# A hybrid decoder trunk: attention two heads at a time between late projections, and the recurrent chain ahead of them

## The chip, the cores and the metric

The kernel runs on one core of a Trainium2 chip. The metric is device time in microseconds for one execution, the median of several runs. The profile is of one further execution. Its engines are TensorE (PE in the rows, PEld its weight loads), VectorE (DVE), ScalarE (ACT), GpSimd (POOL) and SyncE (SP), which here only issues DMAs.

## The reference, cut to what matters

Two layers on a residual stream x of 512 positions by 1024 channels, all in fp32:

```python
for l in range(2):
    x = x + 0.5 * swiglu_ffn(x, ...)            # 1024 -> 2816 -> 1024
    p = rms_norm(x, mix_norm[l]) @ w_in[l]      # split in four groups of heads
    y_a = pool_mixer(p_a, ...)                  # causal means over 2, 4, 8, 16 positions
    y_b = rwkv7_mixer(p_b, ...)                 # recurrence over the 512 positions, 4 heads of 64
    y_c = nsa_mixer(p_c, ...)                   # compressed, selected and windowed attention, 4 heads
    y_d = short_conv_mixer(p_d, ...)            # gated convolution of width 3
    x = x + concat[y_a, y_b, y_c, y_d] @ w_out[l]
    x = x + 0.5 * swiglu_ffn(x, ...)
```

With 512 positions all eight blocks of 64 are selected, so the selected and the windowed attention are both plain causal attention, with keys of their own.

## The kernel before

Activations lie with channels on the 128 partitions and positions along the free dimension. Every large matrix product takes fp32 operands as a high and a low part: `split` loads a weight tile of 128x1024, ScalarE casts it to the high part (L203), VectorE subtracts for the low part (L204), and `mm3` (L206) issues three matmuls of 128x128 by 512 columns for each of the eight chunks of 128 channels (L209 to L211). A weight load (L193) brings two such tiles into one of two buffers.

The feed-forward halves (`ffn`) are dense in such matmuls. The mixers stand between them. `tilep(i)` computes one of 21 projections of 128 output channels, 24 matmuls, into a PSUM bank, mostly one of the two "d" banks. The order of NAMES is: eight for the recurrence (0 to 7), five for attention (8 to 12), two for the pool (13, 14), six for the convolution (15 to 20).

The order of the instructions is made by a planner before the run: it simulates the engines and at each step issues, of the instructions that are ready in its simulation, the one with the lowest priority number. Numbers grow in the order of the program; `at(off, ...)` sets another start for what it calls. Each engine then works strictly in the planned order. The parts and where they stand in it:

- `Rwkv.prep` (L755), once for each half of the heads, prepares the recurrence, in program order.
- `solve` (L924) builds per chunk of 64 positions the triangular matrices M (L936, L938), sends them through DRAM (L944, L946), substitutes on VectorE (L953 to L958), sends the result back (L963, L968) and merges blocks with small matmuls (L983 to L1014), 32x32 and 64x64. Offset 0 from p0, which is the start of the mixers plus 600.
- `chain` (L813) goes through eight chunks one after another: matmuls L824 and L827, a copy on ScalarE (L830), L836, copies on ScalarE and VectorE (L837, L838), L846, and the new state on VectorE (L857). `out` (L861) normalizes four chunks and puts the result into the split output yh, yl (`put`, L452). Offsets 300 and 500.
- `nsa` (L508) prepares the attention, `compress` (L612) with its matmuls L623 among it. Then 32 units, (block of 128 queries, pair of heads j, head in the pair hp, branch br), go through `scores` (L540: matmul L545, minimum on VectorE L548, exponential on ScalarE L551, scaling on ScalarE L555) and, one unit later, `values` (L558: transposes L562, copy L564, matmuls L574). The last unit of a pair of heads puts its output (L577). Offset 2000.
- `filler` holds the pool and convolution projections (13 to 20) with their work and the splits of chunks 0, 1, 6 and 7. Offset 3000.

At the end the output projection (`mix`, L353 to L363) takes the eight chunks of yh, yl in order, while x is reloaded by DMAs on POOL's queue (L354).

Of the kernel before, what the change touches and what calls it, by code (L numbers as in the profile page):

```python
# [98 lines left out]
class Net:  # L99
    PRI = (0, 0, 300, 2000, 3000)  # L100
# [105 lines left out]
    def mm3(self, ps, wh, wl, xh, xl, n, first=True, last=True):  # L206
        for k in range(n):
            sl = slice(k * P, (k + 1) * P)
            self.nc.tensor.matmul(ps, wh[:, sl], xh[:, k], start=(first and k == 0), stop=False)  # L209
            self.nc.tensor.matmul(ps, wh[:, sl], xl[:, k], start=False, stop=False)  # L210
            self.nc.tensor.matmul(ps, wl[:, sl], xh[:, k], start=False, stop=(last and k == n - 1))  # L211
# [108 lines left out]
    def mix(self, h, win, wout, cmpk, cmpv, g):  # L320
# [61 lines left out]
    def mixers(self, tilep, cmpk, cmpv):  # L382
# [4 lines left out]
        p0 = base + 600  # L387
        PR = self.PRI
# [3 lines left out]
        def at(off, fn, *a):  # L392
            save = self.tc.cur_priority
            self.tc.cur_priority = p0 + off
# [4 lines left out]
        def take(i, ps):  # L399
# [7 lines left out]
            if "L0" in sh and "L1" in sh and "rw" not in st:  # L407
                st["rw"] = Rwkv(self, sh)
            for j in range(2):
                if all(n in sh for n in ("L0", "L1", f"k{j}", f"r{j}", f"v{j}")) and j not in st:  # L410
                    st[j] = 1
                    st["rw"].prep(j)
            if all(n in raw for n in ("KV", "q0", "q1", "KS", "VS")) and "L1" in sh and "u" not in st:
                st["u"] = at(PR[1], self.nsa, raw, sh["L1"], cmpk, cmpv) if PR[1] else self.nsa(raw, sh["L1"], cmpk, cmpv)
# [20 lines left out]
        at(PR[4], filler)  # L435

# [13 lines left out]
        self.tc.cur_priority = p0 + 10000  # L450

# [56 lines left out]
    def nsa(self, raw, L1, cmpk, cmpv):  # L508
# [31 lines left out]
        def scores(i, j, hp, br):  # L540
            w, h = P * (i + 1), 2 * j + hp
            hs = slice(64 * hp, 64 * hp + 64)
            kt = KS if br == hp else KW
            pq = self.pd()
            nc.tensor.matmul(pq[:, :w], Q[j][hs, i * P:(i + 1) * P], kt[hs, :w], start=True, stop=True)  # L545
            sc = self.ring()
            mx = self.small(1, "mx", bufs=4)
            nc.vector.tensor_tensor_reduce(sc[:, :w], pq[:, :w], c["bias"][:, S - w:S],  # L548
                                           -(2.0 ** (-2 * (h + 1))), 3.0e38, ALU.add, ALU.min, mx)
            sm = self.small(1, "sum", bufs=4)  # L550
            nc.scalar.activation(sc[:, :w], sc[:, :w], AF.Exp, bias=mx, scale=-1.0, accum_out=sm)  # L551
            cf = self.small(1, "cf", bufs=4)
            nc.vector.reciprocal(cf, sm)
            nc.vector.tensor_mul(cf, cf, gh[:, i, h, 1 + br:2 + br])
            nc.scalar.activation(sc[:, :w], sc[:, :w], AF.Copy, scale=cf)  # L555
            return sc

        def values(sc, i, j, hp, br):  # L558
            w = P * (i + 1)
            ptr = self.pn()  # L560
            for b in range(i + 1):
                nc.tensor.transpose(ptr[:, b * P:(b + 1) * P], sc[:, b * P:(b + 1) * P], self.ident)  # L562
            pT = self.ring()
            nc.scalar.copy(pT[:, :w], ptr[:, :w])  # L564
            if hp == 0 and br == 0:
# [13 lines left out]
        def run():  # L579
            prev = None  # L580
# [10 lines left out]
    def cmp_blocks(self, KV):  # L591
# [3 lines left out]
        for which in range(2):  # L595
# [9 lines left out]
            blk = self.mt(f"cblk{which}", [P, 16, 31])  # L605
# [6 lines left out]
    def compress(self, Q, cmpk, cmpv, gh):  # L612
        nc = self.nc
        v, c = self.v, self.c
        hid = []
        for which, src in ((0, cmpk), (1, cmpv)):
            blk = self.blocks[which]
            ph = self.pn()
            for l4 in range(4):
                w1 = self.ring()  # L620
                nc.sync.dma_start(w1, src[:, 4 * l4:4 * l4 + 4].rearrange("p a b -> p (a b)"))
                for l in range(4 * l4, 4 * l4 + 4):
                    nc.tensor.matmul(ph[0:31, 0:P], blk[:, l], w1[:, (l % 4) * P:(l % 4 + 1) * P],  # L623
                                     start=(l == 0), stop=(l == 15))
            x = self.mt("gx", [32, P])
            u = self.mt("gu", [32, P])
            nc.gpsimd.memset(x, 0.0)
            nc.scalar.copy(x[0:31], ph[0:31, 0:P])
            nc.vector.tensor_mul(u, x, x)
            nc.vector.tensor_scalar(u, u, GELU_A, 1.0, ALU.mult, ALU.add)  # L630
            nc.vector.tensor_mul(u, u, x)
            nc.scalar.activation(u, u, AF.Tanh, scale=GELU_B)
            nc.vector.tensor_scalar(u, u, 0.5, 0.5, ALU.mult, ALU.add)
            nc.vector.tensor_mul(u, u, x)
            pt = self.pn()
            nc.tensor.transpose(pt[:, 0:32], u, self.ident[0:32, 0:32])
            hT = self.mt(f"hT{which}", [P, 4, 32])
            for r in range(1 if which == 0 else 4):
                nc.scalar.copy(hT[:, r], pt[:, 0:32])
            hid.append(hT)  # L640
# [52 lines left out]
    def conv(self, j, tilep, i):  # L693
        nc = self.nc
        cw = self.v["conv"]
        pc = tilep(i)
        ct = self.uring()[:, :S]
        nc.vector.tensor_mul(ct, pc, self.rs)
        nc.gpsimd.tensor_mul(ct, ct, self.rs)
        pu = tilep(i + 1)  # L700
        z = self.uring()[:, :S + 2]
        nc.gpsimd.memset(z[:, 0:2], 0.0)
        nc.vector.tensor_mul(z[:, 2:], ct, pu)
        t = self.yt(6 + j)
        nc.scalar.activation(t, z[:, 0:S], AF.Copy, scale=cw[:, j:j + 1])
# [445 lines left out]
```

## Time and profile before

| | us |
|---|---|
| median of 3 runs | 2085.72 |
| lowest, highest | 2083.14, 2086.73 |
| the profiled execution | 2084.97 |
| its span, first to last instruction | 2083.2 |
| TensorE busy | 2057.5 (99%) |
| VectorE busy | 998.2 (48%) |
| ScalarE busy | 683.3 (33%) |
| GpSimd busy | 258.7 (12%) |

Matmuls are pipelined and their ends are modelled, so a row's duration is longer than the time to the next row's start; prices of matmuls are read here from start to start. A plain fp32 matmul shows two records, one of the split products shows one, a transpose one. The granted clock is a share of the full 2.4 GHz.

### The profile page before, as it was taken

How to read it: one execution, taken by the hardware profiler on the slowest of the kernel's cores; microseconds unless marked ns; L12 is line 12 of the kernel's file. 1: busy time of each engine (PE TensorE's matmuls, PEld its weight loads, DVE VectorE, ACT ScalarE, POOL GpSimd, SP SyncE). 2: the span in 40 equal slices, each digit the busy share in tenths (PEclk: the TensorE clock that was granted, in tenths of full speed). 3: DMA queues.
4: the chain of work that ended last, by engine and by line, in shares of the span. 5: the costliest groups of instructions: out<-in, count | busy, mean ns of one | idle time of the engine just before them, and what ended most of it. 6: DMA issues, size and time to landing. Idle time of an engine off the chain costs nothing.

```text
span 2083.2 us, 25358 instructions
## 1 busy us (share of the span) xinstructions
PE 2057.5 (99%) x10262; PEld 1660.9 (80%) x10262; DVE 998.2 (48%) x1792; ACT 683.3 (33%) x1101; POOL 258.7 (12%) x249
## 2 busy tenths in 40 slices
PE   8999999999999999999999999999999999999999
PEld 6888888778667888888888888887786688888887
DVE  5434445567555443443544344356674544344433
ACT  4322223331464322232333223233324643222221
POOL 1110111113001110011011001110130011100110
PEclk9999999999799999999999999999996999999999
DMA  5223223324103222322322232242250032223223
GB/s 197 94 90 104 100 89 129 117 68 111 63 1 102 90 101 84 109 101 82 110 95 88 87 108 98 84 144 86 92 129 22 1 101 101 94 84 114 86 91 98
DMA packets 60438, 195.20 MB, mean 94 GB/s; under 512 B 29344, under 2 KB 29472, under 8 KB 45600
## 3 DMA queue, kind: packets, MB, share of 16 engines
q1 hardware_dynamic: 57760, 185.18, 27.4%
q0 software_dynamic: 2560, 8.39, 1.1%
q8 instruction: 80, 1.31, 0.3%
q14 instruction: 38, 0.31, 0.0%
HBM read 183.58 MB, written 8.93 MB: 92 GB/s over the span
## 4 chain that ended last, share of the span: by engine, by line
PE 97%; DVE 2%; ACT 0%; issue 0%; DMA 0%; SPq 0%; DVEq 0%
PE d L209 15%; PE d L211 15%; PE d L210 15%; PE r L211 8%; PE r L209 8%; PE r L210 8%; PE n L211 5%; PE n L209 5%; PE n L210 5%; PE o L574 2%; PE d L545 2%; PE n L562 1%; PE r L936 1%; PE n L623 1%; PE c L827 1%; PE c L824 0%
## 5 line engine op out<-in xcount | busy, mean ns | idle before, releaser
L203 ACT CAST wh<-w 128x1024 fp32r<-128x1024 f32 (+2 forms) x360 | 344.3, 956 | 1086.4 <-issue 327.2
L204 DVE TENSOR_TENSOR wl<-w,wh 128x1024 fp32r<-128x1024 f32 (+2 forms) x360 | 400.7, 1113 | 218.5 <-ACT wh L203 211.5
L209 PE MATMUL d<-hh,wh 128*128 128x512 f32 x1008 | 396.9, 394 | 6.9 <-ACT hh L216 6.9
L210 PE MATMUL d<-hl,wh 128*128 128x512 f32 x1008 | 395.7, 393 | 2.7 <-DVE hl L217 2.7
L211 PE MATMUL d<-hh,wl 128*128 128x512 f32 x1008 | 394.9, 392 | 0.0
L210 PE MATMUL r<-hl,wh 128*128 128x512 f32 x736 | 287.0, 390 | 0.0
L211 PE MATMUL r<-hh,wl 128*128 128x512 f32 x736 | 286.8, 390 | 0.0
L209 PE MATMUL r<-hh,wh 128*128 128x512 f32 x736 | 286.8, 390 | 0.0
L270 POOL TENSOR_TENSOR al<-t,ah 128x512 fp32r<-128x512 f32 x88 | 152.6, 1734 | 1062.6 <-ACT ah L269 1062.6
L209 PEld LDWEIGHTS d<-hh,wh 128*128 128x128 f32 x1008 | 189.7, 188 | 49.9 <-ACT hh L216 6.9
L210 PEld LDWEIGHTS d<-hl,wh 128*128 128x128 f32 x1008 | 189.8, 188 | 44.2 <-DVE hl L217 5.3
L211 PEld LDWEIGHTS d<-hh,wl 128*128 128x128 f32 x1008 | 189.8, 188 | 41.3 <-issue 2.3
L264 DVE TENSOR_TENSOR t<-d,rs 128x512 f32<-128x512 f32 x88 | 60.5, 691 | 267.3 <-PE d L211 261.6
L268 DVE TENSOR_TENSOR t<-t,r 128x512 f32<-128x512 f32 x88 | 60.6, 688 | 220.9 <-PE r L211 220.7
L211 PEld LDWEIGHTS r<-hh,wl 128*128 128x128 f32 x736 | 138.2, 188 | 28.6
L209 PEld LDWEIGHTS r<-hh,wh 128*128 128x128 f32 x736 | 138.2, 188 | 28.6
L210 PEld LDWEIGHTS r<-hl,wh 128*128 128x128 f32 x736 | 138.2, 188 | 28.5
L211 PE MATMUL n<-ah,wl 128*128 128x512 f32 x352 | 137.1, 389 | 0.0
L209 PE MATMUL d<-ah,wh 128*128 128x512 f32 x352 | 137.1, 389 | 0.0
L209 PE MATMUL n<-ah,wh 128*128 128x512 f32 x352 | 137.0, 389 | 0.0
L210 PE MATMUL d<-al,wh 128*128 128x512 f32 x352 | 137.0, 389 | 0.0
L211 PE MATMUL d<-ah,wl 128*128 128x512 f32 x352 | 137.0, 389 | 0.0
(297 smaller groups left out, 2343.9 us busy)
## 6 DMA issues: line engine op xcount, KB each, us to landing
w<-in_g SPq DMA_DIRECT2D x87, 1024.0 KB, 4.8
w<-in_d SPq DMA_DIRECT2D x64, 704.0 KB, 4.0
w<-in_win SPq DMA_DIRECT2D x20, 1024.0 KB, 4.9
w<-in_wout SPq DMA_DIRECT2D x8, 1024.0 KB, 5.8
xd<-x POOLq DMA_DIRECT2D x16, 256.0 KB, 4.2
x<-xd POOLq DMA_DIRECT2D x16, 256.0 KB, 5.8
x<-in_x SPq DMA_DIRECT2D x8, 256.0 KB, 5.1
s<-in_cmpk SPq DMA_DIRECT2D x8, 256.0 KB, 3.4
```

The costliest lines, as they stand in the source:

```text
L203: self.nc.scalar.copy(hi, w)
L204: self.nc.vector.tensor_sub(lo, w, hi.bitcast(F32))
L209: self.nc.tensor.matmul(ps, wh[:, sl], xh[:, k], start=(first and k == 0), stop=False)
L210: self.nc.tensor.matmul(ps, wh[:, sl], xl[:, k], start=False, stop=False)
L211: self.nc.tensor.matmul(ps, wl[:, sl], xh[:, k], start=False, stop=(last and k == n - 1))
L264: nc.vector.tensor_mul(t, pg, self.rs)
L268: nc.vector.tensor_mul(th, th, pu)
L270: nc.gpsimd.tensor_sub(al, th, ah.bitcast(F32))
L545: nc.tensor.matmul(pq[:, :w], Q[j][hs, i * P:(i + 1) * P], kt[hs, :w], start=True, stop=True)
L562: nc.tensor.transpose(ptr[:, b * P:(b + 1) * P], sc[:, b * P:(b + 1) * P], self.ident)
L574: nc.tensor.matmul(po["o"][64 * hp:64 * hp + 64], VT[:, b, br * 64:br * 64 + 64], pT[:, b * P:(b + 1) * P], start=False, stop=(br == 1 and ...
L623: nc.tensor.matmul(ph[0:31, 0:P], blk[:, l], w1[:, (l % 4) * P:(l % 4 + 1) * P], start=(l == 0), stop=(l == 15))
```

## The change

It rearranges the mixers. The priorities: the recurrence's parts get offsets from -6000 to -3000 from the start of the mixers, so that they go ahead of all else that is ready; attention and the late projections get one common offset, 2600. The late projections are cut in eight pieces (two of the pool, three for each half of the convolution), and one piece stands behind every second unit of attention. A unit of attention is now two heads: 16 units, each with two score matmuls side by side (partitions 0 to 63 and 64 to 127, a "d" bank each) and values alternating between the two heads' output partitions. The scaling of the scores moves from ScalarE to VectorE. In `compress` the key and the value matmuls alternate, and their activation is computed once for both; in `solve` the two heads of a pair alternate. The outputs of attention and of the recurrence go to tiles of their own, in buffers used before for other things, and all are split at the end in the order 0, 1, 6, 7, 4, 5, 2, 3, in which the output projection takes them. The scratch rings "s" (4) and "u" (4) become one of 8.

```diff
-    def mm3(self, ps, wh, wl, xh, xl, n, first=True, last=True):
-        for k in range(n):
+    def mm3(self, ps, wh, wl, xh, xl, n, first=True, last=True, order=None):
+        for i, k in enumerate(order or range(n)):
...
-            self.mm3(ps, *w2, self.yh, self.yl, NCH)
+            self.mm3(ps, *w2, self.yh, self.yl, NCH, order=(0, 1, 6, 7, 4, 5, 2, 3))
...
-    PRI = (0, 0, 300, 2000, 3000)
+    EARLY, LATE = -6000, 2600
...
             if "L0" in sh and "L1" in sh and "rw" not in st:
-                st["rw"] = Rwkv(self, sh)
+                st["rw"] = at(self.EARLY, Rwkv, self, sh)
...
-                    st["rw"].prep(j)
+                    at(self.EARLY + 500 * (j + 1), st["rw"].prep, j)
...
-        at(PR[0], rw.solve)
-
-        def filler():
-            for j in range(2):
-                self.pool(j, tilep(13 + j))
-            for j in range(2):
-                self.conv(j, tilep, 15 + 3 * j)
-            self.yh = self.hp.tile([P, NCH, S], F32R, tag="hh", name=self.nm("yh"))
-            self.yl = self.hp.tile([P, NCH, S], F32R, tag="hl", name=self.nm("yl"))
-            for c in (0, 1, 6, 7):
-                self.put(c, slice(0, S), self.y[c])
-
-        at(PR[4], filler)
+        at(self.EARLY + 1500, rw.solve)
...
-        at(PR[2], chain, 0)
-        at(PR[2] + 200, chain, 1)
+        at(self.EARLY + 2500, chain, 0)
+        at(self.EARLY + 3000, chain, 1)

         def rest():
-            for _ in units:
-                pass
-
-        at(PR[3], rest)
+            pieces = [lambda: self.pool(0, tilep(13)), lambda: self.pool(1, tilep(14))]
+            for j in range(2):
+                pieces += self.conv(j, tilep, 15 + 3 * j)
+            for k, _ in enumerate(units):
+                if k % 2 == 0:
+                    pieces[k // 2]()
+            self.yh = self.hp.tile([P, NCH, S], F32R, tag="hh", name=self.nm("yh"))
+            self.yl = self.hp.tile([P, NCH, S], F32R, tag="hl", name=self.nm("yl"))
+            for c in (0, 1, 6, 7, 4, 5):
+                self.put(c, slice(0, S), self.y[c])
+            for g in range(2):
+                for c in (2, 3):
+                    self.put(c, slice(256 * g, 256 * g + 256), self.y[c][:, 256 * g:256 * g + 256])
+
+        at(self.LATE, rest)
...
+    def uring(self):
+        return self.mt("s", [P, 16 + S], bufs=8)
+
     def ring(self):
-        return self.mt("s", [P, S], bufs=4)
-
-    def uring(self):
-        return self.mt("u", [P, 16 + S], bufs=4)
+        return self.uring()[:, :S]
...
-        units = [(i, j, hp, br) for i in range(4) for j in range(2) for hp in range(2) for br in range(2)]
+        units = [(i, j, br) for i in range(4) for j in range(2) for br in range(2)]
...
+            pq = [self.pd(), self.pd()]
+            for hp in range(2):
+                hs = slice(64 * hp, 64 * hp + 64)
+                kt = KS if br == hp else KW
+                nc.tensor.matmul(pq[hp][:, :w], Q[j][hs, i * P:(i + 1) * P], kt[hs, :w], start=True, stop=True)
...
-            nc.scalar.activation(sc[:, :w], sc[:, :w], AF.Copy, scale=cf)
+                nc.vector.tensor_scalar(sc[:, :w], sc[:, :w], cf, None, ALU.mult)
...
             for b in range(i + 1):
-                nc.tensor.matmul(po["o"][64 * hp:64 * hp + 64], VT[:, b, br * 64:br * 64 + 64],
-                                 pT[:, b * P:(b + 1) * P], start=False, stop=(br == 1 and b == i))
-            if hp == 1 and br == 1:
-                self.put(4 + j, slice(i * P, (i + 1) * P), po["o"])
+                for hp in range(2):
+                    nc.tensor.matmul(po["o"][64 * hp:64 * hp + 64], VT[:, b, br * 64:br * 64 + 64],
+                                     pTs[hp][:, b * P:(b + 1) * P], start=False, stop=(br == 1 and b == i))
+            if br == 1:
+                nc.scalar.copy(self.y[4 + j][:, i * P:(i + 1) * P], po["o"])
...
+        ph = self.pn()
+        for l4 in range(4):
...
+            for l in range(4 * l4, 4 * l4 + 4):
+                for k in range(2):
+                    nc.tensor.matmul(ph[32 * k:32 * k + 31, 0:P], self.blocks[k][:, l],
+                                     w1[k][:, (l % 4) * P:(l % 4 + 1) * P], start=(l == 0), stop=(l == 15))
...
-        for j in range(2):
-            net.put(2 + j, ts_, t[:, 256 * j:256 * j + 256])
+        if g == 0:
+            self.y = net.mt("T16", [P, 2, S])
+            net.y[2], net.y[3] = self.y[:, 0], self.y[:, 1]
+        nc.vector.tensor_mul(self.y[:, :, ts_], t.rearrange("p (j s) -> p j s", j=2),
+                             pg.rearrange("p (j s) -> p j s", j=2))
...
-            for hp in range(2):
-                hs = slice(64 * hp, 64 * hp + 64)
-                for g in range(2):
-                    pm = net.pr()
-                    for i in range(4):
-                        ch = 4 * g + i
-                        nc.tensor.matmul(pm[:, i * P:(i + 1) * P], AK[j][hs, ch].rearrange("p a b -> p (a b)"),
+            for g in range(2):
+                pm = [net.pr(), net.pr()]
+                for i in range(4):
+                    ch = 4 * g + i
+                    for hp in range(2):
+                        hs = slice(64 * hp, 64 * hp + 64)
+                        nc.tensor.matmul(pm[hp][:, i * P:(i + 1) * P], AK[j][hs, ch].rearrange("p a b -> p (a b)"),
```

## Rows read from the trace of the kernel before

**Rows 1.** The page: busy times, granted clock by slice, the last chain.

```profile
PE 2057.5 (99%) x10262; PEld 1660.9 (80%) x10262; DVE 998.2 (48%) x1792; ACT 683.3 (33%) x1101; POOL 258.7 (12%) x249
PEclk9999999999799999999999999999996999999999
PE 97%; DVE 2%; ACT 0%; issue 0%; DMA 0%; SPq 0%; DVEq 0%
```

**Rows 2.** Busy time by stretch: us, engine busy (records), clock, DMA share, GB/s.

```profile
100.00:150.00 50.00, 50.00 (x222) 41.45 (x221) 18.98 (x24) 13.89 (x18) 6.75 (x4) 1.00 0.24 79
378.00:541.00 163.00, 158.88 (x956) 126.45 (x954) 109.88 (x232) 52.74 (x87) 30.06 (x52) 1.00 0.33 96
541.00:571.00 30.00, 29.00 (x252) 20.23 (x252) 12.52 (x55) 12.86 (x43) 0.00 (x0) 0.55 0.10 36
571.00:640.00 69.00, 68.31 (x525) 45.86 (x525) 39.71 (x175) 45.16 (x122) 0.00 (x0) 1.00 0.03 9
1408.00:1571.00 163.00, 158.90 (x956) 126.49 (x954) 109.86 (x233) 52.75 (x87) 30.02 (x52) 1.00 0.33 96
1571.00:1612.00 41.00, 40.34 (x299) 27.37 (x300) 15.47 (x69) 17.11 (x56) 0.00 (x0) 0.50 0.08 27
1612.00:1675.00 63.00, 62.30 (x478) 41.81 (x477) 36.63 (x160) 41.17 (x108) 0.00 (x0) 1.00 0.00 1
```

**Rows 3.** TensorE's waits from 378 to 640 us: total, times, longest.

```profile
PE r L1003 <- DVE T L993: 1.9, 1, 1.9
```

**Rows 4.** TensorE's timeline (start, us, operation, records): chain, low and full clock.

```profile
560.10 0.69 PE L827 MATMUL c<-sav,M 64*64 64x64 f32 x4
560.71 0.69 PE L824 MATMUL c<-H,KR 128*64 128x128 f32 x2
...
580.32 0.44 PE L827 MATMUL c<-sav,M 64*64 64x64 f32 x4
580.69 0.43 PE L824 MATMUL c<-H,KR 128*64 128x128 f32 x2
```

**Rows 5.** TensorE's timeline: L983 in alternating corners, then narrow scores.

```profile
530.06 1.15 PE L983 MATMUL r<-T,t 64*64 64x64 f32 x32
531.14 0.69 PE L990 MATMUL r<-t,TT 32*32 32x32 f32 x32
531.76 0.49 PE L545 MATMUL d<-KS,q 64*128 64x128 f32 x2
532.18 1.13 PE L736 MATMUL n<-u,mat 128*128 128x512 f32 x2
```

**Rows 6.** TensorE's timeline: values and the widest scores.

```profile
626.10 1.09 PE L574 MATMUL o<-s,VT 128*64 128x128 f32 x8
627.12 1.12 PE L545 MATMUL d<-KW,q 64*128 64x512 f32 x2
628.17 1.09 PE L562 MATMUL n<-cst,s 128*128 128x128 f32 x8
```

**Rows 7.** Groups by line and shape, 395 to 680 us: us, mean ns.

```profile
L936 PE MATMUL r<-KR,AK 64*128 64x128 f32 x64 | 9.0, 283 | 0.0
L623 PE MATMUL n<-s,cblk 128*31 128x128 f32 x64 | 7.4, 273 | 0.0
```

**Rows 8.** TensorE's timeline: L846 alternates column halves.

```profile
615.55 0.45 PE L846 MATMUL c<-sav,AK 128*64 128x64 f32 x8
615.83 0.40 PE L877 MATMUL r<-sav,M 128*64 128x64 f32 x4
```

**Rows 9.** Groups by line and shape, 378 to 684 us: scaling.

```profile
L764 DVE TENSOR_SCALAR t<-t 128x512 f32<-128x512 f32 x2 | 0.8, 424 | 1.2 <-ACT t L763 1.2
...
L555 ACT ACTIVATE s<-s,cf 128x512 f32<-128x512 f32 x8 | 5.5, 714 | 0.0
```

**Rows 10.** Busy time by stretch, ten us of the first part.

```profile
500.00:510.00 10.00, 10.00 (x61) 8.40 (x61) 9.48 (x31) 2.10 (x4) 2.23 (x4) 1.00 0.13 50
```

**Rows 11.** Waits of SP's DMA queue, 378 to 660 us.

```profile
SPq L963 <- DVE t L958: 13.1, 1, 13.1
```

More of the change, by code (lines that the diff above doesn't have):

```diff
@@ L204, in cut @@
         self.nc.vector.tensor_sub(lo, w, hi.bitcast(F32))
-    def mm3(self, ps, wh, wl, xh, xl, n, first=True, last=True):
-        for k in range(n):
+    def mm3(self, ps, wh, wl, xh, xl, n, first=True, last=True, order=None):
+        for i, k in enumerate(order or range(n)):
             sl = slice(k * P, (k + 1) * P)
-            self.nc.tensor.matmul(ps, wh[:, sl], xh[:, k], start=(first and k == 0), stop=False)
+            self.nc.tensor.matmul(ps, wh[:, sl], xh[:, k], start=(first and i == 0), stop=False)
             self.nc.tensor.matmul(ps, wh[:, sl], xl[:, k], start=False, stop=False)
-            self.nc.tensor.matmul(ps, wl[:, sl], xh[:, k], start=False, stop=(last and k == n - 1))
+            self.nc.tensor.matmul(ps, wl[:, sl], xh[:, k], start=False, stop=(last and i == n - 1))
     def feed(self, c, g, h, square=True):
@@ L386, in mixers @@
         base = self.tc.cur_priority
-        p0 = base + 600
-        PR = self.PRI
         raw = {}
@@ L393, in at @@
             save = self.tc.cur_priority
-            self.tc.cur_priority = p0 + off
+            self.tc.cur_priority = base + off
             r = fn(*a)
@@ L558, in values, with scores @@
-        def values(sc, i, j, hp, br):
-            w = P * (i + 1)
[L560 to L565, printed above, removed]
+        def scores(i, j, br):
+            w = P * (i + 1)
+            pq = [self.pd(), self.pd()]
[3 more added lines that the diff above has]
+                nc.tensor.matmul(pq[hp][:, :w], Q[j][hs, i * P:(i + 1) * P], kt[hs, :w], start=True, stop=True)
+            out = []
+            for hp in range(2):
+                h = 2 * j + hp
+                sc = self.ring()
+                mx = self.small(1, "mx", bufs=4)
+                nc.vector.tensor_tensor_reduce(sc[:, :w], pq[hp][:, :w], c["bias"][:, S - w:S],
+                                               -(2.0 ** (-2 * (h + 1))), 3.0e38, ALU.add, ALU.min, mx)
+                sm = self.small(1, "sum", bufs=4)
+                nc.scalar.activation(sc[:, :w], sc[:, :w], AF.Exp, bias=mx, scale=-1.0, accum_out=sm)
+                cf = self.small(1, "cf", bufs=4)
+                nc.vector.reciprocal(cf, sm)
+                nc.vector.tensor_mul(cf, cf, gh[:, i, h, 1 + br:2 + br])
+                nc.vector.tensor_scalar(sc[:, :w], sc[:, :w], cf, None, ALU.mult)
+                out.append(sc)
+            return out
@@ L566, in values @@
+        def values(scs, i, j, br):
+            w = P * (i + 1)
+            pTs = []
+            for hp in range(2):
+                ptr = self.pn()
+                for b in range(i + 1):
+                    nc.tensor.transpose(ptr[:, b * P:(b + 1) * P], scs[hp][:, b * P:(b + 1) * P], self.ident)
+                pT = self.ring()
+                nc.scalar.copy(pT[:, :w], ptr[:, :w])
+                pTs.append(pT)
+            if br == 0:
                 if j == 0:
@@ L604, in cmp_blocks @@
                 nc.gpsimd.tensor_copy(two[64:, 0:S - 1], own[:, 1:S])
-            blk = self.mt(f"cblk{which}", [P, 16, 31])
+            blk = self.mt(f"cblk{which}", [P, S])[:, :496].rearrange("p (l n) -> p l n", n=31)
             st = two.rearrange("p (n l) -> p l n", l=16)
@@ L614, in compress @@
         v, c = self.v, self.c
[L615 to L640, printed above, removed]
@@ new lines, in compress @@
+        x = self.mt("gx", [64, P])
+        u = self.mt("gu", [64, P])
+        nc.gpsimd.memset(x, 0.0)
+        for k in range(2):
+            nc.scalar.copy(x[32 * k:32 * k + 31], ph[32 * k:32 * k + 31, 0:P])
+        nc.vector.tensor_mul(u, x, x)
+        nc.vector.tensor_scalar(u, u, GELU_A, 1.0, ALU.mult, ALU.add)
+        nc.vector.tensor_mul(u, u, x)
+        nc.scalar.activation(u, u, AF.Tanh, scale=GELU_B)
+        nc.vector.tensor_scalar(u, u, 0.5, 0.5, ALU.mult, ALU.add)
+        nc.vector.tensor_mul(u, u, x)
@@ L641, in compress @@
+        pt = self.pn()
+        nc.tensor.transpose(pt[:, 0:64], u, self.ident[0:64, 0:64])
+        hid = [self.mt("hT0", [P, 1, 32]), self.mt("hT1", [P, 4, 32])]
+        nc.scalar.copy(hid[0][:, 0], pt[:, 0:32])
+        for r in range(4):
+            nc.scalar.copy(hid[1][:, r], pt[:, 32:64])
         pk = self.pn()
```

67 lines of the change are left out of this document (32 added, 35 removed).

## The prediction, made from the trace of the kernel before

> **What bounds the kernel now.** I read the page first. TensorE is busy for 99% of the span and carries 97% of the chain that ended last, so time is only won by giving TensorE less work, or the same work at a better rate; the granted clock is full except in two spots of the 40 slices [rows 1]. Those spots are the mixers, one per layer, so next comes the table by stage [rows 2]. The reader should see three things in it. (a) A stretch of feed-forward gives the dense rate: 222 matmuls of 512 columns in 50 us, 0.225 us each. (b) Each layer's mixers have a first part (163 us, 956 records) that holds all 21 input projections, and a second part (99 us in layer 0, 104 us in layer 1, 777 records each) in which the DMAs move nearly nothing: no projection is left there, only attention and the recurrent chain. The eight pool and convolution projections, though last by priority, were used up earlier. (c) The clock falls in the second part: 0.55 over 30 us and 0.50 over 41 us, before it is 1.00 again. With the two levels 1.0 and 0.5 (2.4 and 1.2 GHz) that is 30 x 0.45 / 0.5 = 27 us and 41 us at half clock.
>
> Visible idle time of TensorE is small: in layer 0 it is (163.0 - 158.9) + (30.0 - 29.0) + (69.0 - 68.3) = 5.8 us, in layer 1 as much [rows 2]; the longest single wait is 1.9 us [rows 3]. Removing waits as such can therefore bring at most some 11 us. What remains are the low clock and the cost of the small matmuls.
>
> **Term 1, the clock.** The change moves the recurrent chain beside projections 8 to 12 and spreads the eight late projections over the attention. The low clock begins where the dense work ends (541 us, 1571 us) and after a run of 32x32 matmuls, so with dense work on both sides I expect it gone. Its price can be read in two ways. The two layers do the same 777 records; layer 1 has 41 - 27 = 14 us more of half clock and takes 104 - 99 = 5 us longer, 0.36 us per us. And one step of the chain, four records of L827, takes 0.61 us at half clock against 0.37 us at full [rows 4]: 39% of the time is lost. So 68 us at half clock cost 68 x 0.36 = 24 us to 68 x 0.39 = 27 us. I take **25 us**. The ends are 0 (the clock stays low elsewhere) and 34 us (half of 68).
>
> **Term 2, two at a time.** Four kinds of small matmul are reordered so that neighbours lie in different halves of the array. Their serial prices now: scores (L545) 0.42 us at 128 columns [rows 5] and 1.05 us at 512 [rows 6], in between 0.63 and 0.84, eight of each per layer: 8 x 2.94 = 23.5 us. Values (L574): 1.02 us for eight records, two records a matmul, so 0.255 us [rows 6]; 80 of them are 20.4 us. KR x AK (L936) takes 9.0 us, the compression (L623) 7.4 us, 32 matmuls each [rows 7]. Together 60.3 us per layer, 121 us in all.
>
> What does a neighbour in another half bring? Before has such orders for other steps. L983 alternates 64x64 corners: 16 matmuls in 1.08 us [rows 5], 68 ns each. L846 alternates column halves: four in 0.28 us, 70 ns each [rows 8]. The non-alternating L827 of the same 64 columns takes 0.37 us for two, 185 ns each [rows 4]. So alternating clearly overlaps something, mostly weight loads; none of these has the shapes of the change. Bounds: 0 (weights and columns of the larger shapes don't overlap) and 50% (two at the price of one; more I exclude, since only two halves alternate). I take 40%, near the upper end, because both rows that do alternate are below half of the one that doesn't. It holds only where the neighbours really stand side by side. For L936 and L623 they should, their operands being all ready: 2 x 16.4 x 0.4 = 13 us. For scores and values each half waits for its own buffer and its own softmax, and the planner issues whichever is ready first; I take half: 2 x 43.9 x 0.4 x 0.5 = 17.5 us. Sum **30 us**; the ends are 0 and 60 us.
>
> A rule speaks against part of this. Scores cost 0.42 us at 128 columns and 1.05 us at 512 [rows 5, 6], a slope of 0.21 us per 128 columns, hence a fixed 0.21 us per visit. The Trainium skill (TensorEngine Tiling (Array Packing), Tiling Modes, Key Properties) says that changing the tiling mode drains the engine, which would explain the fixed part, and the change puts eight full-array projections per layer between tiled scores. If each adds two such switches, 8 x 2 x 0.21 x 2 layers = 7 us come on top by my estimate, and the sum would be 7 us higher; I leave it out, since a planner that filled gaps with projections before made such switches too.
>
> **Term 3, waits removed.** Of the 11 us of visible idle time I take half, **6 us**: the solve's waits (1.9 us, [rows 3]) then lie beside projections. Ends 0 and 11 us.
>
> **What the change costs.** (i) A pair of scores takes both "d" banks, and so does a late projection take one of them; after each piece the second score waits for VectorE's eviction. The nearest row of that size on VectorE is 0.42 us [rows 9]; with the hand-overs before and behind it I take 1 us, 16 pieces in both layers, 16 us if nothing covers it. Behind that score wait the transposes of its own pair, but the values of the pair before are ready by then; I charge half, **8 us**, ends 0 and 16 us. (ii) The scaling of scores goes from ScalarE, 0.71 us at 512 columns, to VectorE; its nearest row is L764, 0.42 us [rows 9], so at most 32 x 0.42 = 13.6 us more on VectorE per layer. TensorE kept 10.00 of 10 us while VectorE was 9.5 of 10 busy [rows 10]; so nothing on the path, and if VectorE fills up, up to 14 us per layer. (iii) All splits of the mixers' outputs now come at the end, chunks 4 and 5 whole. Behind the last value matmul stand a copy, a cast and a subtraction, by the 0.71 and 0.42 us of [rows 9] about 2 us a layer; the output projection begins with the chunks 0, 1, 6, 7, which are 12 matmuls x 0.225 = 2.7 us for the first output and more for the next three banks. **2 us**, ends 0 and 8 us. The reload of x, issued on POOL's queue, starts later by the same few us and is needed only by the additions to x. (iv) The solve's nine small DMAs per layer are moved in SP's queue ahead of weight loads. One of them waited 13.1 us for VectorE's substitution [rows 11], and a weight load behind it waits too. Two weight buffers hold four projections, 4 x 24 x 0.225 = 21.6 us of dense work, so nothing; if that cover is gone, 13 us per layer. (v) On POOL the solve's masks go ahead of the attention's preparation, the eight scratch buffers are now shared, and the outputs reuse buffers whose readers are long done: nothing, covered by projections.
>
> **Sum.** The profiled execution took 2084.97 us (span 2083.2 us and 1.8 us around it), 0.75 us under the median of 2085.72 us. 25 + 30 + 6 - 8 - 2 = 51 us, so 2085 - 51 = **2034 us** for a profiled execution and for the median alike, 2.4% faster.
>
> **Rivals.** A: *everything pairs and covers*. The upper ends, 34 + 60 + 11 = 105 us, less some tail: about 1985 us. For it: the pairs share operands and nearly the same moment. Against: scores and values are issued by readiness. I take 2000 us as its middle. B: *the late projections are used up early again*, as in (b), because attention's preparation is slow and the planner needs fillers then; attention ends alone and the clock falls in it once more. Then only the pairs of L936 and L623 (13 us) and some of the others pay: about 2062 us. For it: exactly this happened before with the lowest priority. Against: the chain now fills that time. C, the other side: *TensorE waits in order for the recurrence*. Its small steps go to the front, each followed by a hand-over to ScalarE or VectorE; if the planner thinks these shorter than they are, TensorE stands. Eight chunks with three hand-overs each at the longest wait of before, 1.9 us [rows 3], are 46 us per layer, 91 us in all: 2034 + 91 = 2125 us. It decides from 51 / 48 = 1.1 us exposed per hand-over. Against it: before had the same planner and steps, and showed 5.8 us of idle time per layer. D: *the change does not do what it says*, pairs do not overlap and dips of the clock remain: 6 - 10 = -4 us, 2089 us, about no change.
>
> **How the numbers follow.** Forecast 0.55 (2012 to 2055 us), A 0.20, B 0.11, C 0.08, D 0.06. About 0.2% (4 us) is what a measurement can tell from no change. Faster: 0.55 + 0.20 + 0.11 = 0.86 and a little of D, 0.87; same 0.04; slower 0.09. The range leaves out C, D and the far end of A: 1990 to 2068 us.
>
> **What would show it.** In the trace after, the granted clock should be 1.00 through both mixers; the second part should hold projections (DMAs moving weights between attention records); the last L836 of a layer should come well before the last scores; score records should start in twos. L623's 64 records should take about 4.4 us instead of 7.4 us. If the clock still falls, term 1 is wrong; if records of a pair start a whole matmul apart, term 2; if idle time before chain steps passes 25 us a layer, C is right.

## The result, and the profile after

| | before | after |
|---|---|---|
| median (after: 4 runs) | 2086.22 | 2105.61 (2105.16 to 2113.70) |
| the profiled execution | 2084.97 | 2105.16 |
| its span | 2083.2 | 2103.4 |

The change makes the kernel slower, by 1%: ratio 1.0104, 95% interval 1.0077 to 1.0131, where 2034 us was predicted. (The median of before is that of the runs timed beside after.)

The page of after, to be read against [rows 1]: busy times, granted clock by slice, and the chain that ended last.

```profile
PE 2049.9 (97%) x10260; PEld 1648.5 (78%) x10260; DVE 1011.2 (48%) x1834; ACT 654.5 (31%) x1039; POOL 253.2 (12%) x247
PEclk9999999986899999999999999999989999999999
PE 94%; DVE 4%; DMA 1%; ACT 1%; issue 1%; SPq 0%; POOL 0%; DVEq 0%; ACTq 0%; POOLq 0%
```

TensorE is busy for 8 us less, but the span is 20 us longer: it now stands, and VectorE has 4% of the chain, where it had 2%. The mixers' stretches of after (columns as in [rows 2]: us, then for TensorE, its weight loads, VectorE, ScalarE and GpSimd the busy time with records, then the clock, DMA share and GB/s) show where.

```profile
378.00:492.00 114.00, 108.77 (x537) 86.68 (x536) 64.92 (x127) 33.78 (x48) 8.82 (x30) 0.88 0.28 90
...
502.00:510.00 8.00, 1.20 (x5) 0.89 (x5) 7.95 (x42) 0.88 (x4) 4.17 (x4) 0.53 0.37 131
510.00:541.00 31.00, 28.19 (x398) 21.66 (x399) 19.61 (x57) 8.61 (x27) 6.48 (x9) 0.78 0.28 44
541.00:571.00 30.00, 29.00 (x155) 19.87 (x156) 11.64 (x43) 9.89 (x29) 1.28 (x1) 0.79 0.06 18
571.00:661.00 90.00, 89.53 (x631) 61.74 (x630) 56.16 (x183) 38.79 (x95) 4.02 (x5) 1.00 0.11 36
...
1534.00:1571.00 37.00, 25.70 (x138) 19.36 (x132) 23.74 (x101) 8.80 (x33) 8.40 (x7) 0.72 0.38 75
```

Before, TensorE was busy for 10.00 of 10 us from 500 to 510 while VectorE worked for 9.48 [rows 10]. After, VectorE works through 7.95 of 8 us and TensorE for 1.20. The second part (571 to 661) does hold projections now and is as full as it was meant to be: 89.53 of 90 us at full clock. TensorE's waits of after, layer 0 (378 to 720 us; total, times, longest; compare [rows 3]):

```profile
PE n L663 <- DVE t L979: 6.5, 1, 6.5
PE r L502 <- ACT t L498: 3.6, 1, 3.6
PE r L1004 <- DMA T<-tdram: 1.8, 2, 1.5
PE d L543 <- DVE mx L549: 1.7, 1, 1.7
PE r L892 <- DVE H L875: 1.0, 1, 1.0
```

Its timeline there (start, us, operation, records, wait before it):

```profile
492.00 0.37 PE L543 MATMUL d<-KS,q 64*128 64x128 f32 x1
492.01 0.37 PE L543 MATMUL d<-KW,q 64*128 64x128 f32 x1
492.21 0.27 PE L543 MATMUL d<-KS,q 64*128 64x128 f32 x1
492.22 0.27 PE L543 MATMUL d<-KW,q 64*128 64x128 f32 x1
492.88 0.50 PE L209 MATMUL d<-hh,wh 128*128 128x512 f32 x1 [0.38 <-DVE mx L549]
...
502.92 0.42 PE L543 MATMUL d<-KW,q 64*128 64x128 f32 x1
509.80 0.28 PE L663 MATMUL n<-cst,kc 32*128 32x32 f32 x1 [6.46 <-DVE t L979]
...
521.17 0.79 PE L209 MATMUL d<-hh,wh 128*128 128x512 f32 x1
```

The first late projection starts at 492.88, as soon as the minimum of the first scores (mx, L549) has given a "d" bank back; the second starts at 521.17. Between them TensorE waits for VectorE's substitution (L979, it was L953 to L958) and the attention's preparation, with no dense work to put there. VectorE's timeline of after names both waits:

```profile
509.39 0.27 DVE L661 TENSOR_SCALAR kc<-kc,krs 32x128 f32<-32x128 f32 x1
509.58 0.18 DVE L979 TENSOR_TENSOR t<-t,t 128x39 f32<-128x39 f32 x1
...
517.76 0.28 DVE L549 CUSTOM_DVE_ANT_0 s<-d,cst 128x128 f32<-128x128 f32 x1
```

L663 transposes kc, the compressed keys, and L661 delivers kc at 509.66 us, in the middle of the substitution; the wait is listed under L979, the step of the substitution beside it. And the scores issued at 502.33 to 502.92 keep both "d" banks until VectorE has come to them at 517.55 and 517.76; only behind that can the second projection start. Before, the first scores came at 531.76 us [rows 5], and the late projections ahead of them. VectorE's timeline of before shows it taking up the results of the last six (L698, L703 and L710, three for each half of the convolution; those of the pool are taken up at 465.55 and 479.17):

```profile
495.01 0.69 DVE L698 TENSOR_TENSOR u<-d,rs 128x512 f32<-128x512 f32 x1 [0.35 <-PE d L211]
502.91 0.68 DVE L703 TENSOR_TENSOR u<-u,d 128x512 f32<-128x512 f32 x1
...
512.04 0.68 DVE L710 TENSOR_TENSOR y<-y,d 128x512 f32<-128x512 f32 x1
516.09 0.69 DVE L698 TENSOR_TENSOR u<-d,rs 128x512 f32<-128x512 f32 x1 [0.42 <-PE d L211]
525.09 0.69 DVE L703 TENSOR_TENSOR u<-u,d 128x512 f32<-128x512 f32 x1 [1.43 <-PE d L211]
...
536.36 0.69 DVE L710 TENSOR_TENSOR y<-y,d 128x512 f32<-128x512 f32 x1 [0.16 <-PE d L211]
```

The dense work of before in 500 to 510 us was therefore late projections.

For the whole change and the experiments I add up, in stretches of 2 us over both mixers, TensorE's visible idle time and the time at half clock, each taken as (1 - clock) / 0.5 x 2 us. With 0.4 us lost per us at half clock (0.36 to 0.39 by the prediction's working; 0.43 by the runs of one program told of below; an estimate), the rest, span - idle - 0.4 x half clock, is the work.

| kernel | span | idle | half clock | work, against before | median, ratio and interval |
|---|---|---|---|---|---|
| before | 2083.2 | 11.3 | 68 | 0 | |
| after | 2103.4 | 40.2 | 96 | -20 | 2105.6, 1.0104 (1.0077 to 1.0131) |
| e1 | 2082.3 | 35.5 | 72 | -27 | 2089.1, 1.0020 (1.0003 to 1.0038) |
| e2 | 2116.0 | 46.9 | 96 | -14 | 2120.1, 1.0184 (1.0157 to 1.0211) |
| e3 | 2079.6 | 14.7 | 38 | +5 | 2082.0, 1.0035 (0.9991 to 1.0080) |
| e4 | 2095.7 | 39.5 | 75 | -18 | 2093.7, 1.0052 (1.0034 to 1.0071) |
| e5 | 2078.8 | 30.4 | 79 | -28 | 2080.3, 0.9984 (0.9966 to 1.0002) |
| e6 | 2058.2 | 17.2 | 79 | -35 | 2076.9, 0.9967 (0.9940 to 0.9995) |
| e7 | 2092.1 | 43.3 | 96 | -34 | 2093.9, 1.0057 (1.0033 to 1.0081) |
| e8 | 2087.4 | 33.1 | 82 | -23 | 2089.9, 1.0021 (1.0005 to 1.0037) |
| e9 | 2115.5 | 39.1 | 119 | -16 | 2118.1, 1.0161 (1.0133 to 1.0190) |
| e10 | 2100.9 | 31.4 | 96 | -13 | 2105.1, 1.0099 (1.0076 to 1.0122) |
| e11 | 2078.2 | 16.3 | 44 | 0 | 2081.7, 1.0000 (0.9977 to 1.0023) |

So of after's +20 us, idle time gives +29, the clock +27 x 0.4 = +11, and the work -20. (In e6 and e7 part of the work is left out.) The median of e3 is that of eight runs, five near 2082 us and three near 2109; two more, at 2137.9 us and a mean granted clock of 0.959, were in a slower state and are left out. Layer 0 loses 17.8 us, layer 1 only 2.5: the clock is worse in layer 0 (61 us at half against 27) and better in layer 1 (34 against 41).

The same two figures by stretch of layer 0, idle time and half clock in us (460 to 530 us holds the solve and the attention's preparation, 571 to 720 us the end of the mixers), show where each kernel stands:

| kernel | late projections ahead of the attention | 460 to 530 us | 571 to 720 us |
|---|---|---|---|
| before | issued early | 1.0, 0 | 0.7, 0 |
| after | 0 | 12.8, 44 | 1.5, 0 |
| e9 | 0, better priority | 12.7, 44 | 1.3, 0 |
| e4 | 4 | 7.5, 15 | 9.1, 10 |
| e8 | 6 | 2.5, 12 | 10.1, 14 |
| e1 | 8 | 3.4, 0 | 9.2, 14 |
| e5 | 8 | 0.4, 0 | 8.8, 14 |
| e6 | 8 | 1.8, 0 | 1.1, 0 |

### The profile page after: what moved, and what is told of

The parts are those of the page before. It is cut to its first block, busy times and chain, and to the rows that moved or that the text cites. A ratio compares the mean times of both kernels' runs of the same rounds, so it can differ in the third digit from the quotient of the medians.

```text
span 2103.4 us, 25284 instructions
## 1 busy us (share of the span) xinstructions
PE 2049.9 (97%) x10260; PEld 1648.5 (78%) x10260; DVE 1011.2 (48%) x1834; ACT 654.5 (31%) x1039; POOL 253.2 (12%) x247
## 4 chain that ended last, share of the span: by engine, by line
PE 94%; DVE 4%; DMA 1%; ACT 1%; issue 1%; SPq 0%; POOL 0%; DVEq 0%; ACTq 0%; POOLq 0%
PE d L209 15%; PE d L210 15%; PE d L211 15%; PE r L209 8%; PE r L211 8%; PE r L210 8%; PE n L209 5%; PE n L211 4%; PE n L210 4%; PE d L543 1%; PE o L580 1%; PE r L956 1%; PE n L566 1%; DVE wl L204 1%; PE c L845 1%
## 5 line engine op out<-in xcount | busy, mean ns | idle before, releaser
L210 PE MATMUL n<-al,wh 128*128 128x512 f32 x352 | 136.9, 389 | 0.0
```

## The experiments

**Where the late projections stand: e1, e4, e8, e9.** The theory: a projection can't be issued before the scores that are written ahead of it in the program, since the "d" banks are handed out in the program's order; so the pieces, set between the units, are lost as cover for the first part. e1 writes all eight ahead of the units; e4 four, e8 six.

```diff
-            for k, _ in enumerate(units):
-                if k % 2 == 0:
-                    pieces[k // 2]()
+            for p in pieces:
+                p()
+            for _ in units:
+                pass
```

> The changed kernel with one thing undone: all eight late projections come ahead of the attention units in the program, so they get their PSUM banks before the scores do. Priorities, pairs and output tiles stay as changed. Cover theory (the change took dense work away from the stretch of about 460 to 522 us in which solve and the attention's preparation wait on VectorE): TensorE's visible idle time falls from about 19 us a layer to about 6 us, the clock stays full until the attention, and the pairs now show as a gain: 2045 to 2070 us. Recurrence-first theory (the recurrence's VectorE work delays the attention's preparation): nothing of it is undone, 2095 to 2106 us. Pair theory (waits for two banks cost more than pairs give): 2085 to 2100 us.

> The changed kernel with the first four late projections ahead of the attention and the other four between its units, one after every second unit. Cover theory: four projections are about 22 us of dense work, close to the 19 us of idle time, so most of the hole closes: 2050 to 2075 us; whether it beats the run with all eight ahead depends on the low clock of the second part. Pair theory: half of the loss stays, about 2080 to 2095 us. Recurrence-first theory: 2095 to 2106 us.

> The changed kernel with six late projections ahead of the attention and the last two behind units 8 and 12. Cover theory: the hole of the first part stays closed (six are 32 us of dense work) and the two fill waits near the end: idle time below the 35 us of both layers in the run with all eight ahead, 2070 to 2088 us. If the planner's spreading of the recurrence costs more than the two give: 2088 to 2096 us.

With 0, 4, 6 and 8 pieces ahead the medians are 2105.6, 2093.7, 2089.9 and 2089.1 us: the first four give the most back, six and eight can't be told apart, and 16.5 us of the loss are gone with all eight. The wait at L663 is gone in e1, and in the table by stretch the hole at 460 to 530 us closes as pieces go ahead. Mixing the late projections into the attention, the change's main idea, costs time here.

The cover theory is right on the hole and wrong on what closing it brings. It expected 2045 to 2070 us of e1 and 2050 to 2075 us of e4, with some 6 us of idle time a layer; both missed, e1 has 18 us of idle time a layer, and 2089.1 and 2093.7 us lie in the ranges of the pair theory. That theory's mechanism isn't seen: in layer 0 of e1 scores wait 0.4 us for a bank, in after 1.7. What the cover theory left out is the right column of the table: with the projections ahead, 9 to 10 us of idle time come up at the end of the mixers, which e6 below takes up. By the sum, e1's span is 21 us shorter than after's: 5 us of idle time, 10 of clock and 7 of work. e8 lies in its second range (2088 to 2096 us).

Whether the place in the program or the priority number holds them back, e9 asks: the pieces keep their place but get a lower number than attention.

```diff
-                    pieces[k // 2]()
+                    at(1500, pieces[k // 2])
```

> The changed kernel with one edit: the eight late pieces keep their place in the program, behind every second unit of attention, but their priority number (1500) is below that of attention (2600), so that a piece that could be issued would go first. Theory buffers by program order: the two d banks are handed out in the order of the program, so piece 0 still waits for the banks of the first scores, whatever its priority; first scores still near 492 us, visible idle near 500 to 510 us stays (some 6 us), 2105 us (2098 to 2112). Rival, priority: the pieces went late because of their numbers; then they fill the first part again as in the run with the late projections first, the hole at 500 to 510 us closes, and the time is near 2089 us.

The waits of e9, same view as above, hold the same hole:

```profile
PE n L663 <- DVE t L979: 6.5, 1, 6.5
...
PE d L543 <- DVE mx L549: 1.7, 1, 1.7
```

First scores at 491.84 us, first piece behind them at 492.72: a priority doesn't bring a projection past a buffer that the program gives to somebody else first. So the theory of the buffers holds on the mechanism; on the time, 2118.1 us, both ranges missed. e9 is 12 us slower than after, which I had not expected; 119 - 96 = 23 us more of half clock are 9 of them, and the rest is not settled.

**The recurrence first: e2, e3, e5.** e2 is after with the recurrence's offsets as before, e3 is before with the early offsets alone, e5 is e1 with the offsets as before, so that pairs, output tiles and rings remain.

```diff
-                st["rw"] = at(self.EARLY, Rwkv, self, sh)
+                st["rw"] = Rwkv(self, sh)
...
-        at(self.EARLY + 1500, rw.solve)
+        at(600, rw.solve)
...
-        at(self.EARLY + 2500, chain, 0)
-        at(self.EARLY + 3000, chain, 1)
+        at(900, chain, 0)
+        at(1100, chain, 1)
```

> The changed kernel with only the recurrence's offsets set back to those of the kernel before (prep in program order, solve 600, chain 900 and 1100). Recurrence-first theory: the attention's preparation ends earlier and the time falls to 2086 us or below. Cover theory: the late projections still stand behind the scores, so 2098 to 2112 us. Pair theory: 2098 to 2112 us too.

> The kernel before with only the recurrence moved ahead of all else (the changed kernel's offsets). Recurrence-first theory: it loses by itself, 2095 us or more. Cover theory: the late projections are still free to fill gaps, so 2080 to 2090 us, no change beyond the spread. The forecast's own idea (an earlier chain shortens the second part) would give 2060 us or less.

> The changed kernel with the late projections ahead of the attention and the recurrence's offsets as before: what stays of the change is the pairs, the scaling on VectorE and the output tiles. From the sums so far (length = matmul work + visible idle time + 0.38 us per us at half clock) the pairs take about 9.5 us of work off each layer. If that gain survives: 2062 to 2072 us. If the recurrence sets the end of the mixers, the attention ends earlier and TensorE waits for the last chunks: 2078 to 2095 us, with idle time and low clock at the end of the mixers.

No single price comes out: undoing it costs 14 us in the changed kernel (e2 against after) and gains 9 us where the late projections go first (e5 against e1); alone it makes no difference that its interval can tell from none (e3). The theory that "recurrence first" made after slow is refuted by e2, at 2120.1 us slower than every range given for it. e3's five executions near 2082 us fit "no change"; the 2060 us of the forecast's own idea is not there. e5 is the shortest kernel here that computes everything: 2080.3 us, and its interval still touches 1. It lies in the second of its ranges: 28 us of work saved by the sum, but 19 us more of idle time and some 10 us more of half clock than before, with a wait of 6.1 us for the recurrence's layer norm at the end of the mixers of each layer. So even with the cover back in place the pairs bring no gain that can be told from none.

Nor did "first" make the recurrence early. Its matmuls KR x AK begin at 468.81 us in after and 469.36 before; the chain's T64 x R steps (L836, now L854) run from 546.4 to 620.9 us before, from 539.6 to 642.3 in after: 14.7 against 10.6 us per chunk, over seven. TensorE's order in after shows why:

```profile
563.30 0.44 PE L845 MATMUL c<-sav,M 64*64 64x64 f32 x4
563.67 0.51 PE L892 MATMUL r<-H,KR 128*64 128x128 f32 x2
564.12 1.22 PE L543 MATMUL d<-KW,q 64*128 64x256 f32 x2
565.26 0.79 PE L209 MATMUL d<-hh,wh 128*128 128x512 f32 x1
...
571.56 0.40 PE L210 MATMUL d<-hl,wh 128*128 128x512 f32 x1
571.79 0.38 PE L577 MATMUL o<-pct,vc 128*128 128x128 f32 x2
572.11 0.43 PE L580 MATMUL o<-s,VT 128*64 128x128 f32 x2
572.47 0.46 PE L854 MATMUL c<-R,TT 64*64 64x64 f32 x8
```

Between a step (L845) and the next of the same chunk (L854), with only one copy on ScalarE between them, stand a score, 17 dense matmuls and values: 8.8 us. Here the plan fills a hand-over of the chain with dense work, and TensorE keeps to the plan.

**What the recurrence holds up: e6, e7.** Both leave out the update of the state between chunks (in before the matmuls L846 and the state on VectorE, L857; the chunks read a state of zero), e6 from e1, e7 from after. A chunk then doesn't wait for the one before.

> The run with the late projections first, with the state update of the recurrence left out (the matmul of AK with sav and the updates of H; every chunk then reads a zero state). That takes some 2 us of TensorE's work and 7 us of VectorE's a layer and cuts the dependence from chunk to chunk. If the recurrence sets the end of the mixers there (the last step L855 of layer 0 starts at 637 us and the attention has ended at 628 us): the wait of 6.1 us and the low clock at 638 to 652 us go, 2060 to 2078 us. If not: 2084 to 2090 us.

> The changed kernel with the same left out. If its second part is full of matmul work (attention, recurrence and the late projections that were moved there), the time falls only by the work taken out: 2094 to 2105 us. If there too the recurrence sets the end (14.7 us from chunk to chunk against 10.6 us before): 2085 us or less.

At the same mean granted clock (0.981 and 0.982) e6's profiled span is 24 us under e1's, and its idle time falls from 35 to 17 us; at equal clock (0.977) e7's is 11 us under after's, with the idle time unchanged (40 and 43 us). The wait that goes away in e6 stands at the end of the mixers of e1 (600 to 660 us):

```profile
PE r L904 <- DVE t L942: 6.1, 1, 6.1
PE d L209 <- ACT yh L451: 1.2, 1, 1.2
```

And the stretch of it, e1's 630 to 655 us, at a granted clock of 0.73:

```profile
630.00:655.00 25.00, 16.30 (x90) 11.00 (x88) 10.53 (x35) 5.24 (x11) 4.36 (x8) 0.73 0.21 63
```

With the late projections early again, attention is over before the recurrence (last values 627.6 us, last chain step 636.6), and `out`'s layer norm on VectorE (L942) then stands alone. So the recurrence sets the end of the mixers in e1, and in after, where it is later still, it is covered by the projections that were moved there. e6's runs spread from 2060.7 to 2087.2 us (median 2076.9, just inside its first range), and the profiled one is the fastest of the ten; at a mean granted clock of 0.975 a run of e6 took 2073.1 us and one of e1 2096.2, 23 us apart too, so the comparison at equal clock is the cleaner one. e7's median of 2093.9 us stands at the lower edge of its first range (2094 to 2105 us), only the work taken out: after's second part is full.

**The scaling on ScalarE: e10.** e5 with the scaling of the scores left there.

```diff
-                nc.vector.tensor_scalar(sc[:, :w], sc[:, :w], cf, None, ALU.mult)
+                nc.scalar.activation(sc[:, :w], sc[:, :w], AF.Copy, scale=cf)
```

> The run with pairs and outputs alone (late projections first, recurrence not first: 2080.3 us) with one more part undone: the scaling of the scores stays on ScalarE. Theory VectorE in the recurrence's way: the 32 scalings add up to 13.6 us a layer to VectorE's queue, and the copies and state updates of the chain stand behind them; without them a chunk of the chain comes sooner (last chain step near 625 us instead of 629.75), and the time falls by 5 to 10 us, to 2070 to 2075 us. Rival, TensorE's own order: the chunks are late because of the dense matmuls and attention that the plan puts between the chain's steps on TensorE; then the last step stays near 630 us and the time within 4 us of 2080 us. Third: ScalarE, which does the softmax, becomes the later one, and it is 5 us slower.

All but the third theory miss, and that one misses by its size: 2105.1 us, 25 us slower than e5, the last chain step at 637.0 instead of 629.75. Of the 22 us of span, 7 are clock (17 us x 0.4) and 1 is idle time; 14 are work. Part of it is seen in the order: in e5's layer 0 two scores of different halves stand side by side in 11 of 16 possible places, in e10's in 7. First e5, a unit with 384 columns, then one with 384 columns in e10:

```profile
573.46 0.59 PE L544 MATMUL d<-KW,q 64*128 64x384 f32 x1
573.47 0.59 PE L544 MATMUL d<-KS,q 64*128 64x384 f32 x1
573.89 0.48 PE L544 MATMUL d<-KW,q 64*128 64x384 f32 x1
573.89 0.48 PE L544 MATMUL d<-KS,q 64*128 64x384 f32 x1
```

```profile
576.12 0.91 PE L544 MATMUL d<-KW,q 64*128 64x384 f32 x2
577.33 0.91 PE L544 MATMUL d<-KS,q 64*128 64x384 f32 x2
```

The next matmul starts at 574.31 in e5, 0.85 us after the first of the four records, and at 576.97 in e10, 0.85 us after the first of only two: a neighbour saves the whole of one score. The four places lost are one score of 128 columns, one of 256 and two of 384, some 2.7 us a layer by the prediction's prices, 5 to 6 us in both layers; where the other 9 are is not settled.

**One pair alone: e11.** Before with the compression of after (the diff's `compress`, and nothing else).

> The kernel before with one part of the change alone: the compression of keys and values as alternating column halves with one activation for both (L623 and what follows it). Theory that the pair's price is real and on the path: 64 records per layer at 57 to 62 ns instead of 113 ns are 3.5 us a layer, 7 us in all, 2079 us, ratio 0.9966. Rival: in the first part TensorE's work only moves the end of attention's preparation, which is bound by VectorE's solve, so less than half of it arrives, 2083 to 2086 us.

Neither expectation can be told from the other: ratio 1.0000 (0.9977 to 1.0023), 12 runs, nine of them from 2079.6 to 2085.9 us and three from 2094.3 to 2099.3. The profiled one has 24 us less of half clock than before, worth more than its whole gain of 5 us; no work saved can be seen in its total. The records themselves did get cheaper, 32 of them in 1.87 us (490.58 to 492.45 us), 58 ns each: a price that holds in the trace and is lost in the total.

## Why the prediction was wrong, point by point

**What bounds the kernel.** Right that TensorE does; wrong in reading (b) as a loss. That the eight late projections had been "used up earlier" was the cover under which VectorE's solve and the attention's preparation ran. The step that failed is in cost (ii) and (iv): "TensorE kept 10.00 of 10 us while VectorE was 9.5 of 10 busy", so "nothing on the path". The row was right; the projections that made it so were the ones the change takes away from there, and the text didn't ask which they were. Cost (iv) even named the condition, "if that cover is gone, 13 us per layer", and put it at nothing. What the runs show in its place: TensorE's idle time between 460 and 530 us of layer 0 goes from 1.0 to 12.8 us, and 44 us of half clock come with it, by the 0.4 above some 18 us. That the projections' absence opens the hole is shown: written ahead again (e1) they close it, and with a better priority alone (e9) they don't.

A second step failed with it: that the chain would run early and be covered. With the late projections back ahead, in e1 and e5, the recurrence sets the end of the mixers (9 us of idle time in layer 0, 1.1 in e6), which is part of why closing the hole alone doesn't bring the forecast gain.

**Term 1, the clock: -25 us predicted, +11 measured.** The second part is at full clock as forecast (571 to 661 us), but the low clock moved forward: the granted clock is 0.53 in the hole and 0.88 over 378 to 492 us, where before had 1.00 to 541 us [rows 2]. Its price per us held: one program, e3, took 2081.5 us at a mean granted clock of 0.990 and 2108.8 us at 0.975; 27.3 us for 0.015 x 2 x 2095 = 63 us of half clock is 0.43.

**Term 2, two at a time: -30 us predicted, -20 measured** (as work, the other edits in it). In e5 it is -28. The values and the compression paid about the 40% or more. In after, values (first fence) and the compression and KR x AK of layer 1 (second), to be read from start to start:

```profile
639.15 1.09 PE L580 MATMUL o<-s,VT 128*64 128x128 f32 x13
640.17 1.09 PE L566 MATMUL n<-cst,s 128*128 128x128 f32 x8
```

```profile
1523.35 1.16 PE L956 MATMUL r<-KR,AK 64*128 64x128 f32 x8
1524.43 0.33 PE L845 MATMUL c<-sav,M 64*64 64x64 f32 x2
...
1528.51 1.29 PE L631 MATMUL n<-s,cblk 128*31 128x128 f32 x20
1529.72 1.16 PE L956 MATMUL r<-KR,AK 64*128 64x128 f32 x8
```

Values are 1.02 / 13 = 78 ns a record (some records may be missing; e5 shows 16 in 1.02 us, 64 ns) against 128 [rows 6]; the compression 1.21 / 20 = 60 ns, against (493.99 - 490.38) / 32 = 113 ns before:

```profile
490.38 3.68 PE L623 MATMUL n<-s,cblk 128*31 128x128 f32 x32
493.99 0.32 PE L827 MATMUL c<-sav,M 64*64 64x64 f32 x2
```

KR x AK takes 1.08 / 8 = 135 ns, as before: "their operands being all ready" was true, but each head writes a bank of its own, and in TensorE's order the four matmuls of one bank (x8 in the rows) stand ahead of the four of the other, so the alternation written in the program never came about. The scores paid where two halves meet (e10's fences), in after in 6 of 16 places of layer 0. But only two of the six are the two heads of one unit, both at 128 columns (492.00 and 502.33 us); in the other four the second head of one unit meets the first of the next, as here, where all four records read KS and a unit reads KS for one head and KW for the other:

```profile
628.66 1.13 PE L543 MATMUL d<-KS,q 64*128 64x512 f32 x4
```

So from 256 columns on every unit's two heads start more than a matmul apart, the sign that the prediction had named against term 2, and that about the assumed share of the scores was saved all the same is luck. Whether the 7 us for switches of the tiling mode that the prediction left out were paid, no run here shows.

The Trainium skill (TensorEngine Tiling (Array Packing), Tiling Modes, Key Properties) says that different tiles of the array load weights and multiply in parallel. The trace agrees where neighbours do lie in different halves, 113 to 60 ns with column halves and 0.85 us for four score records of 384 columns instead of two with row halves. That the halves must also be neighbours in the executed order is what KR x AK and e10's scores add.

**Term 3, waits: -6 us predicted, +29 measured.** The old waits were small; new ones came in the first part of each layer: 6.5 us at L663 in layer 0, 6.4 in layer 1, and 3.6 us at L502, where the recurrence's preparation goes ahead of projections (1.4 us in e2 and e5, where it doesn't).

**Costs (i) and (iii).** The bank hand-over is there, 1.7 + 0.5 us ("DVE mx L549") in layer 0, less than the 4 us charged; the tail shows a wait of 0.4 us in layer 1, where 1 us a layer was charged. What (i) missed is not the price of a hand-over but its order: the bank decides when a projection may start at all.

**The rivals.** B came out the other way round: the late projections were not used early enough. C had the sign, and its 2125 us stood 19 us above the result, D's 2089 us 17 us below it; but C's mechanism is not what happened. Idle time stayed under its 25 us a layer (20), and the waits named are for VectorE's solve and the attention's preparation, hardly for the recurrence's state (1.0 us at L892). Of what the prediction said would show it, the full clock through both mixers failed (0.53 in the hole), the records starting in twos failed but for two units a layer, and "the last L836 of a layer should come well before the last scores" failed: 642.3 against 646.1 us, the chain's own cadence having gone from 10.6 to 14.7 us. The projections in the second part came, and L623's 64 records came out at or below the 4.4 us forecast (60 ns each, 3.9 us).

## What to carry to other kernels

Before work is moved away from where it was used up early, look at which engine was busy there and name the very instructions that covered it: here the filler was worth most beside the stretch that another engine bounds, and closing one hole brought up the next, at the end of the mixers. A priority doesn't reorder what a shared buffer orders, so a filler that takes its bank behind an attention unit in the program comes behind it on the chip. And pairs for different halves of the array paid about half here only where they were neighbours in the executed order, which is to be read there, not in the source.

## What was not expected of the hardware

One and the same program (e3) took 2081.4 to 2082.1 us in five executions, at a mean granted clock of 0.990, and 2108.7 to 2110.6 us in three others, at 0.975. The same instructions thus differ by 27 us with the granted clock, more than half of the 51 us that all the edits here were meant to bring, and one profiled execution doesn't tell which of such levels a kernel will mostly have. What decides between them within one program is not settled.
